# Second token half ahead of a norm by 512-column products, and the first high weight parts behind low ones 192 bytes off in a line

## The chip, the cores and the metric

The kernel runs on one core of one Trainium2 chip. The metric is device time in microseconds, the median over timed executions of the whole kernel. The core has a matrix engine (PE, with its weight loads shown as PEld), a vector engine (DVE), a scalar engine (ACT), GpSimd (POOL) and SyncE (SP), which issues most DMA transfers. PE reads its operands from SBUF and writes sums to PSUM, which has eight banks of 2 KB per partition; DVE and ACT read them from there.

## What is computed

A two-layer decoder over 256 tokens of 2048 values, in float32: a Mamba-2 layer, then an attention layer, each followed by a gated feed-forward block, and after each of the four a normalisation:

```python
def layer_norm(x, g, b):
    xf = x.astype(jnp.float32)
    mu = jnp.mean(xf, axis=-1, keepdims=True)
    var = jnp.mean(jnp.square(xf - mu), axis=-1, keepdims=True)
    return ((xf - mu) * lax.rsqrt(var + LN_EPS) * g + b).astype(x.dtype)

def conv_ffn(x, w_up, conv_w, conv_b, w_down):
    u = causal_dwconv(x @ w_up, conv_w, conv_b)
    gate, val = u[..., :D_FF], u[..., D_FF:]
    return (jax.nn.silu(gate) * val) @ w_down

    for layer in range(DEPTH):
        ...
        h = layer_norm(DEEPNORM_ALPHA * h + mix, ln_mix_g[layer], ln_mix_b[layer])
        ffn = conv_ffn(h, ffn_w_up[layer], ffn_conv_w[layer], ffn_conv_b[layer], ffn_w_down[layer])
        h = layer_norm(DEEPNORM_ALPHA * h + ffn, ln_ffn_g[layer], ln_ffn_b[layer])
```

`mix` ends in a product with `w_out` (Mamba-2) or `w_o` (attention). So each of the four norms stands behind a product into 2048 columns: `mamba_w_out` (4096 rows), `ffn_w_down` (5632 rows, twice) and `attn_w_o` (2048 rows).

## The kernel before

**Products in high and low parts.** Weights and activations are float32. A weight tile `raw` is split into a high part `hi` (ACT casts it to the rounded type that PE multiplies, L209) and the rest `lo = raw - hi` (DVE, L210). Activations are kept in the same two parts (`hT`, `yT`, `gT`, `aT`). A product is hi x hi + hi x lo + lo x hi, all added up in PSUM.

**Chunks and steps.** The weights of all layers are cut into chunks of 512 columns, and a chunk into steps; one step is one 512 KB tile. SP loads tiles in order into four `raw` buffers. `split` (L182) makes the two parts of a tile and asks for the load of another tile. There are four `hi` and four `lo` buffers, so a split waits until PE is done with an older step. PE works through the steps in an order written out by hand; other work is hung on it by `at`, `amid`, `within` and `beyond` (after a step, in its middle, within or after one half's products).

**W chunks** hold the weights still in PE. `some` (L250) goes through a step's `hi` part with 512 moving columns (L267: activations' high and low part beside each other, `x.both(k)`) and through its `lo` part with 256 (L270: the high part alone). Two steps in a row share a change: one has hi, then lo, the next lo, then hi (`kinds`, L157); in paired chunks hi, hi, lo, lo and then lo, lo, hi, hi. So PE's stream is runs of 16 or 32 L267 products and runs as long of L270 products.

**X chunks**, among them those ahead of the norms, hold the activations still and move the weights. `half(i, t, piece)` (L221) makes the products of step `i` for token half `t` (128 tokens): hi x hi (L231), hi x lo (L232), lo x hi (L236), for two row blocks, 6 products with 512 columns.

**Ahead of a norm** stand four X chunks, 512 columns each. In the last one, chunk 3, the second token half is made in two pieces of 256 columns (`second`, L239, calls `half(i, 1, 0)` and `half(i, 1, 1)`), for all its steps. Each piece has a PSUM tile of its own. The last 4 steps (TAIL; 8 in the last norm, LAST) are the tail: the first half is finished for all of them, then piece 0 for all of them, then piece 1. So the norm of the first half starts while PE works on the pieces, and that of the second half's first columns while PE works on piece 1. The chunk's first two steps (head) put both first halves ahead of both second ones. In the first three norms the weight parts of the tail's last three steps lie in `hT` (`spare`), which is free then, and the steps split behind them belong to the next chunk.

**The norm** (`class Norm`): `r` holds the residual, four tiles of 2 x 512 columns. `add` (L448) computes `r = ALPHA * r + product` on DVE out of PSUM and takes statistics; `stats` sums them up; `center` and `scale` (DVE), or `all_off` (ACT and POOL), apply them; `turn` transposes the result into `hT` by PE (L407), ACT (L411) and DVE (L412).

**Places in SBUF.** A line is 64 floats, 256 bytes. `hT`, `yT`, `gT`, `aT`, all `hi` tiles and the `lo` tiles of X chunks begin at one place in a line, called 0 here. The `lo` tiles of W chunks begin 192 bytes further (the `gap` tile lies between) and have a stretch of 32 floats between their halves, so that their weights lie at 192 and 64 in turns of two products.

**PSUM**: three `acc` tiles of two banks and two `tp` tiles of one bank. Chunk 3 has one `acc` tile for its first half, and for the pieces the first banks of the other two (in the last norm, the two `tp` tiles).

Of the kernel before, what the change touches and what calls it, by code (L numbers as in the profile page):

```python
# [18 lines left out]
F32 = mybir.dt.float32  # L19
F32R = mybir.dt.float32r  # L20
AF = mybir.ActivationFunctionType
OP = mybir.AluOpType
AX = mybir.AxisListType

P = 128
# [11 lines left out]
ALPHA = 4.0 ** 0.25  # L37
LN_EPS = 1e-5
RMS_EPS = 1e-5
NC = 512  # L40
HC = NC // 2
NEG = -1.0e30
LINE = 64
# [12 lines left out]
LAST = 8  # L56
# [35 lines left out]
def yoco_kernel(ctx: ExitStack, tc: tile.TileContext, x, lmg, lmb, lfg, lfb, x_t, columns, w, out):  # L92
    nc = tc.nc
# [10 lines left out]
    def acc_pair():  # L104
        return psum.tile([P, 2, NC], F32, tag="acc", name="acc", bufs=3)

    def tp_tile():
        return psum.tile([P, NC], F32, tag="tp", name="tp", bufs=2)
# [1 line left out]

    ident = base.tile([P, P], F32, name="ident")
    make_identity(nc, ident)
    mean = base.tile([P, P], F32R, name="mean")


    cols = base.tile([P, -(-N_COL // LINE) * LINE], F32, name="cols")
# [9 lines left out]
    steps, plan = [], chunks()  # L126

    class Chunk:

# [40 lines left out]
    def load():  # L172
# [6 lines left out]
            nc.sync.dma_start(t[:, e], w[i][:, e])  # L179
        raw_t[i] = t  # L180

    def split():  # L182
        i = pos["split"]
        pos["split"] += 1
        t = raw_t.pop(i)
        if i in spare:
            h, l = (bufs["h"][:, k:k + 2].rearrange("p k a t -> p k (a t)") for k in (spare[i], spare[i] + 2))
        else:
            h = wts.tile([P, 2, NC], F32R, tag="hi", name="hi")
            if not gap:  # L190
                gap.append(wts.tile([P, LINE * 3 // 4], F32R, tag="gap", name="gap", bufs=1))
            l = wts.tile([P, 2 * NC + LINE], F32R, tag="lo", name="lo")
            if len(gap) < 2:
                gap.append(wts.tile([P, LINE // 4], F32R, tag="gap2", name="gap2", bufs=1))
            if steps[i][0].mode == "W":
                l = l.rearrange("p (a n) -> p a n", a=2)[:, :, :NC]
            else:
                l = l[:, LINE // 4:LINE // 4 + 2 * NC].rearrange("p (a n) -> p a n", a=2)
        hi_t[i], lo_t[i] = h, l
        if steps[i][0].mode == "H":  # L200
            for a, w in enumerate((h, l)):
                v = t[:, a].rearrange("p (k n) -> p k n", k=8)
                w = w.rearrange("p a (k e n) -> p (a k) e n", e=2, n=NC // 8)
                nc.scalar.copy(w[:, :, 0], v)
                nc.vector.tensor_sub(w[:, :, 1], v, w[:, :, 0].bitcast(F32))
            return load()
        for e in ((0,), (1,)) if i < 2 else ((0, 1),):
            sl = slice(e[0], e[-1] + 1)
            nc.scalar.copy(h[:, sl], t[:, sl])  # L209
            nc.vector.tensor_sub(l[:, sl], t[:, sl], h[:, sl].bitcast(F32))  # L210
        load()
# [9 lines left out]
    def half(i, t, piece=None):  # L221

        ch, s = steps[i]
        h, l = hi_t[i], lo_t[i]
        sl = slice(0, NC) if piece is None else slice(piece * HC, (piece + 1) * HC)
        a = ch.part[t] if piece is None else ch.piece[piece]
        ts = slice(t * P, (t + 1) * P)
        for kk in range(2):
            k = 2 * s + kk
            th = ch.x.hi(k)[:, ts]  # L230
            nc.tensor.matmul(a, th, h[:, kk, sl], start=k == 0, stop=False)  # L231
            nc.tensor.matmul(a, th, l[:, kk, sl], start=False, stop=False)  # L232
        run(inner, (i, t, piece))
        for kk in range(2):
            k = 2 * s + kk
            nc.tensor.matmul(a, ch.x.lo(k)[:, ts], h[:, kk, sl], start=False, stop=k == ch.nk - 1)  # L236
        run(outer, (i, t, piece))

    def second(i):  # L239

        if steps[i][0].tail:
            half(i, 1, 0)
            half(i, 1, 1)
        else:
            half(i, 1)

    def done(i):
        hi_t.pop(i), lo_t.pop(i)
# [61 lines left out]
    def products(i):  # L310
        ch, s = steps[i]
        if ch.mode == "W":
            if s == 0:
                ch.part = []
            if s == 0 or (not ch.both and s == ch.n // 2):
                ch.part += [acc_pair() for _ in range(1 + ch.both)]
        elif s == 0:
            a = acc_pair()
            ch.part = [a[:, 0, :], a[:, 1, :]] if ch.mode == "X" else [a]
            if ch.tail:  # L320
                ch.part.pop()
                ch.piece = [tp_tile()[:, :HC] if ch.tail == LAST else acc_pair()[:, 0, :HC] for _ in range(2)]
        if ch.mode != "X":
            return whole(i)
        half(i, 0)
        if i >= ch.end - ch.tail:
            if i < ch.last:
                return splits(i)
            for q in range(2):
                for j in range(ch.end - ch.tail, ch.end):  # L330
                    half(j, 1, q)
                    if q:
                        done(j)
        elif s < ch.head - 1:
            if ch.tail:
                splits(i)
        elif s == ch.head - 1:
            for j in range(ch.first, i + 1):
                if j < i or ch.tail:
                    splits(i, 1)  # L340
                second(j)
                done(j)
        else:
            run(mid, i)
            splits(i)
            second(i)
            done(i)

    post, pre, mid, inner, outer = {}, {}, {}, {}, {}
# [11 lines left out]
    def amid(i, f, *a):  # L361
        mid.setdefault(i, []).append((f, a))
# [5 lines left out]
    def beyond(i, t, q, f, *a):  # L368

        outer.setdefault((i, t, q), []).append((f, a))  # L370
# [52 lines left out]
    class Norm:  # L423
# [24 lines left out]
        def add(self, c, h, q=None):  # L448
            r = self.r[c][:, h]
            if q is None:  # L450
                nc.vector.scalar_tensor_tensor(r, r, ALPHA, self.chs[c].part[h], op0=OP.mult, op1=OP.add)
            else:
                v = r[:, q * HC:(q + 1) * HC]
                nc.vector.scalar_tensor_tensor(v, v, ALPHA, self.chs[c].piece[q], op0=OP.mult, op1=OP.add)
            for w in (0, 1) if q is None else (q,):
                nc.vector.bn_stats(self.st[:, h, 2 * c + w, :], r[:, w * HC:(w + 1) * HC])

        def add2(self, c):
            for h in range(2):
# [133 lines left out]
    yT = bufs["y"] = mp.tile([P, DI // P, 2, S], F32R, name="yT")  # L593
    BT = mp.tile([P, NG, S], F32, name="BT")
    CT = mp.tile([P, NG, S], F32, name="CT")
    tri = base.tile([P, P], F32, name="tri")
    nc.gpsimd.memset(tri, 1.0 / NC)
    nc.vector.tensor_copy(mean, tri)
    nc.gpsimd.memset(tri, 1.0)
# [319 lines left out]
    def chain(norm, nxt=None, after=None):  # L919

        chs = norm.chs
        last = chs[3].last
        at(chs[0].first, norm.open)
        for c in range(4):
            at(max(chs[0].first, chs[c].last - 7), norm.fetch, c)
            if c < 3:
                at(chs[2].first + 3 + c, norm.fetch_gb, c)
                amid(chs[c].end, norm.add2, c) if c < 2 else beyond(chs[2].end, 0, None, norm.add2, c)
        beyond(last, 0, None, norm.add, 3, 0)
        beyond(last, 0, None, norm.stats, 0)  # L930
        if not nxt:
            return
        beyond(last, 0, None, norm.center, 0, 0)
        beyond(last, 1, 0, norm.scale, 0, 0)
        for e in range(SPARE):
            spare[last - SPARE + 1 + e] = 4 + 4 * e
        n = nxt.first

        def turn(c, h):
            turn_half(norm.r, c, h)  # L940

        beyond(last, 1, 0, norm.all_off, 1, 0)
        beyond(last, 1, 0, norm.add, 3, 1, 0)
        beyond(last - 2, 1, 1, turn, 0, 0)
        beyond(last, 1, 1, norm.add, 3, 1, 1)
        beyond(last, 1, 1, norm.stats, 1)
        beyond(last, 1, 1, norm.center, 0, 1)
        beyond(n, 0, None, norm.scale, 0, 1)
        beyond(n, 0, None, turn, 1, 0)
        beyond(n + 1, 0, None, norm.fetch_gb, 3)  # L950
        beyond(n + 1, 0, None, norm.center, 1, 1)
        beyond(n + 1, 0, None, norm.scale, 1, 1)
        within(n + 2, 0, None, turn, 0, 1)
        beyond(n + 2, 0, None, norm.all_off, 2, 0)
        beyond(n, 1, None, turn, 1, 1)
        beyond(n, 1, None, norm.center, 2, 1)
        beyond(n, 1, None, norm.scale, 2, 1)
        beyond(n + 1, 1, None, norm.all_off, 3, 0)
        beyond(n + 2, 1, None, turn, 2, 0)
        beyond(n + 2, 1, None, norm.center, 3, 1)  # L960
        beyond(n + 3, 0, None, turn, 2, 1)
        beyond(n + 3, 0, None, norm.scale, 3, 1)
        beyond(n + 4, 0, None, turn, 3, 0)
        beyond(n + 4, 1, None, turn, 3, 1)
        for c in range(4):
            at(n + 3 + c, norm.store, c)
        at(n + 6, after)
# [188 lines left out]
    def rest(h):  # L1156
# [9 lines left out]
        for q in range(2):  # L1166
            n3.norm(3, h, slice(q * HC, (q + 1) * HC))

    beyond(end, 0, None, n3.gb_psum, 3)
    beyond(end, 0, None, rest, 0)  # L1170
    beyond(end, 1, 0, n3.add, 3, 1, 0)
# [47 lines left out]
```

## Time and profile before

| | |
|---|---|
| median of 3 executions | 2513.02 us (2512.54 to 2513.26) |
| profiled execution, its own time | 2512.1 us |
| its span from first to last instruction | 2509.8 us |
| PE, PEld busy | 2497.9, 2170.8 us |
| DVE, ACT, POOL busy | 1657.9, 1365.5, 76.4 us |
| DMA | 502.59 MB, mean 200 GB/s |

A row of a timeline gives start and duration in us, engine, line, operation, what is written and read by the program's names, the shape, how many instructions follow each other, and in brackets how long the engine had been idle before and what ended that. A row of the chain of waits gives start, time and what it was. Ends of matmuls are modelled, so their pace is read from starts.

### The profile page before, as it was taken

What the parts mean: (1) busy time and instruction counts of PE and PEld (TensorE: products, weight loads), DVE (VectorE), ACT (ScalarE), POOL (GpSimd) and SP (SyncE); (2) the same over time, 40 slices, a digit from 0 to 9 for tenths busy, and PEclk for the clock granted to TensorE, in tenths of its full rate; (3) what the DMA queues carried; (4) which work ended last, traced back from release to release, by engine and by line L of the source; (5) the groups of instructions that cost most, each with busy time, mean ns of one, the idle gap of its engine ahead of it and who ended that gap; (6) DMA issues with size and microseconds to landing.
All of it is one profiled execution on the core that took longest, in us unless ns stands there. A gap on an engine that the chain in (4) does not pass through costs nothing.

```text
span 2509.8 us, 36085 instructions
## 1 busy us (share of the span) xinstructions
PE 2497.9 (100%) x13983; PEld 2170.8 (86%) x13983; DVE 1657.9 (66%) x2140; ACT 1365.5 (54%) x1790; POOL 76.4 (3%) x96
## 2 busy tenths in 40 slices
PE   9999999999999999999999999999999999999998
PEld 8888888888888888888888888888888888888887
DVE  7878888755676767675445646645767676765445
ACT  6677787643465655554334445543556555554333
POOL 0000000000200000000000200000200000000001
PEclk9999999999999999999999999999999999999999
DMA  7666655666666556656666665456666556566674
GB/s 260 207 189 205 209 191 190 205 210 220 215 203 193 193 193 193 194 185 202 210 229 204 210 193 175 161 176 227 221 192 197 194 191 194 187 200 201 199 228 161
DMA packets 141739, 502.59 MB, mean 200 GB/s; under 512 B 15856, under 2 KB 16368, under 8 KB 141568
## 3 DMA queue, kind: packets, MB, share of 16 engines
q1 hardware_dynamic: 136448, 482.92, 59.3%
q0 software_dynamic: 4832, 16.85, 2.2%
q8 instruction: 109, 1.79, 0.3%
q14 instruction: 62, 0.51, 0.1%
q10 hardware_dynamic: 288, 0.52, 0.1%
HBM read 491.77 MB, written 8.45 MB: 199 GB/s over the span
## 4 chain that ended last, share of the span: by engine, by line
PE 99%; DMA 0%; DVE 0%; SPq 0%; issue 0%; ACT 0%
PE acc L267 41%; PE acc L270 20%; PE acc L231 11%; PE acc L232 11%; PE acc L236 11%; PE acc L805 1%; PE tp L407 0%; PE tp L236 0%; PE tp L232 0%; PE tp L231 0%; DMA raw<-in_w 0%; PE tp L814 0%; PE acc L788 0%; PE tp L1084 0%; PE tp L1118 0%; PE tp L1110 0%
## 5 line engine op out<-in xcount | busy, mean ns | idle before, releaser
L210 DVE TENSOR_TENSOR lo<-raw,hi 128x1024 fp32r<-128x1024 f32 (+1 forms) x869 | 1060.0, 1225 | 722.6 <-ACT hi L209 596.4
L209 ACT CAST hi<-raw 128x1024 fp32r<-128x1024 f32 (+1 forms) x869 | 909.0, 1049 | 826.8 <-PE acc L236 366.6
L267 PE MATMUL acc<-hT,hi 128*128 128x512 f32 x4480 | 1059.0, 391 | 0.4 <-DVE hT L570 0.3
L267 PEld LDWEIGHTS acc<-hT,hi 128*128 128x128 f32 x4480 | 826.9, 188 | 165.0 <-ACT hi L209 0.9
L270 PEld LDWEIGHTS acc<-hT,lo 128*128 128x128 f32 x4480 | 538.6, 188 | 15.6 <-issue 1.2
L270 PE MATMUL acc<-hT,lo 128*128 128x256 f32 x4480 | 544.6, 277 | 0.0
L232 PE MATMUL acc<-lo,gT 128*128 128x512 f32 (+1 forms) x678 | 254.5, 378 | 0.0
L231 PE MATMUL acc<-hi,gT 128*128 128x512 f32 (+1 forms) x678 | 254.1, 377 | 0.0
L236 PE MATMUL acc<-hi,gT 128*128 128x512 f32 (+1 forms) x678 | 200.7, 377 | 0.0
L232 PEld LDWEIGHTS acc<-lo,gT 128*128 128x128 f32 x678 | 127.7, 188 | 23.3
L231 PEld LDWEIGHTS acc<-hi,gT 128*128 128x128 f32 x678 | 127.6, 188 | 23.1
L236 PEld LDWEIGHTS acc<-hi,gT 128*128 128x128 f32 x678 | 124.9, 188 | 23.6
L232 PE MATMUL acc<-lo,yT 128*128 128x512 f32 (+1 forms) x270 | 98.6, 369 | 0.0
L231 PE MATMUL acc<-hi,yT 128*128 128x512 f32 (+1 forms) x270 | 98.5, 369 | 0.0
L231 PE MATMUL acc<-hi,hT 128*128 128x512 f32 x192 | 78.8, 410 | 0.0
L236 PE MATMUL acc<-hi,yT 128*128 128x512 f32 (+1 forms) x270 | 77.7, 369 | 0.0
L232 PE MATMUL acc<-lo,hT 128*128 128x512 f32 x192 | 75.4, 393 | 0.0
L610 DVE TENSOR_TENSOR u<-u,acc 128x512 f32<-128x512 f32 x108 | 73.5, 681 | 2.3 <-ACT u L609 1.4
L637 DVE SCALAR_TENSOR_TENSOR g<-u,cols,g 128x254 f32<-128x254 f32 (+1 forms) x176 | 73.3, 478 | 2.4 <-ACT g L632 2.4
L1034 ACT CAST gT<-v 128x512 fp32r<-128x512 f32 x44 | 27.3, 621 | 84.5 <-DVE v L1033 84.5
L637 DVE SCALAR_TENSOR_TENSOR v<-u,cols,v 128x254 f32<-128x254 f32 (+1 forms) x176 | 73.2, 478 | 0.0
L469 POOL TENSOR_TENSOR rs<-rs,mhalf 128x1 f32<-128x1 f32 x8 | 7.4, 930 | 1982.1 <-DVE nb L470 1982.1
(223 smaller groups left out, 1911.3 us busy)
## 6 DMA issues: line engine op xcount, KB each, us to landing
raw<-in_w SPq DMA_DIRECT2D x880, 512.0 KB, 3.8
mA<-acum_d POOLq DMA_DIRECT2D x16, 512.0 KB, 6.1
hres<-r POOLq DMA_DIRECT2D x12, 512.0 KB, 7.1
r<-hres SPq DMA_DIRECT2D x12, 512.0 KB, 4.6
eA<-acum_d POOLq DMA_DIRECT2D x16, 128.0 KB, 7.5
r<-in_x SPq DMA_DIRECT2D x4, 512.0 KB, 5.8
gb<-in_ln_mix_g SPq DMA_DIRECT2D x8, 256.0 KB, 4.7
gb<-in_ln_mix_b SPq DMA_DIRECT2D x8, 256.0 KB, 4.9
```

The lines of the kernel that those rows point to most:

```text
L209: nc.scalar.copy(h[:, sl], t[:, sl])
L210: nc.vector.tensor_sub(l[:, sl], t[:, sl], h[:, sl].bitcast(F32))
L231: nc.tensor.matmul(a, th, h[:, kk, sl], start=k == 0, stop=False)
L232: nc.tensor.matmul(a, th, l[:, kk, sl], start=False, stop=False)
L236: nc.tensor.matmul(a, ch.x.lo(k)[:, ts], h[:, kk, sl], start=False, stop=k == ch.nk - 1)
L267: nc.tensor.matmul(banks[j], w[:, a, b, js], ch.x.both(k), start=begins, stop=ends, skip_group_check=True)
L270: nc.tensor.matmul(banks[j][:, :S], w[:, a, b, js], ch.x.hi(k), start=begins, stop=ends, skip_group_check=True)
L469: nc.gpsimd.tensor_tensor(self.rs[:, h, :], self.rs[:, h, :], mhalf[:, 0, :], op=OP.pow)
L610: nc.vector.tensor_add(dst, dst, p[:, :, :S])
L637: nc.vector.scalar_tensor_tensor(d, u[:, i % 2, :S - k], c1(self.at_w, w[n - 1 - k] + self.ia + i), d, op0=OP.mult, op1=OP.add)
L805: nc.tensor.matmul(ps[64 * q:64 * q + 64, c, j * P:(j + 1) * P], G[g]["xdt"][:, c, h * 64:(h + 1) * 64], G[g]["A", c][:, h, :], start=True ...
L1034: nc.scalar.copy(h, v[:, sl])
```

## The change

1. In chunk 3 ahead of a norm, the steps before the tail make their second half with one 512-column product in place of two of 256 columns, into a bank of their own (`ch.part[1]`): in the first three norms the second bank of piece 0's `acc` tile, in the last one the second bank of the first half's tile. The pieces sum up the tail's steps only (`k0` and `k1` say where a sum starts and ends).
2. `add_most` adds that bank to `ALPHA * r`, by a DVE instruction of 512 columns; `add` of a piece adds the piece alone. In the first three norms it stands behind the first half of the tail's last step but one, in the last norm behind the first half's sum and statistics.
3. `hi` tiles are 64 floats longer. For a W step whose `hi` part starts an L267 run behind an L270 run (`behind`), its first half lies at 192 and its second half at 0.
4. `tri` and `mean`, 512 bytes each, move from one pool to another, which makes room for the longer tiles.

```diff
-    mean = base.tile([P, P], F32R, name="mean")
...
+    def behind(i):
+
+        ch, s = steps[i]
+        if ch.mode != "W" or (ch.paired and s % 2):
+            return False
+        if ch.kinds(s)[0] == 1:
+            return True
+        ch, s = steps[i - 1]
+        return i > 0 and ch.mode == "W" and ch.kinds(s)[1] == 1
+
...
-            h = wts.tile([P, 2, NC], F32R, tag="hi", name="hi")
+            h = wts.tile([P, 2 * NC + LINE], F32R, tag="hi", name="hi")
+            if behind(i):
+                h = h[:, LINE // 2:].rearrange("p (a n) -> p a n", a=2)[:, :, LINE // 4:]
+            else:
+                h = h[:, :2 * NC].rearrange("p (a n) -> p a n", a=2)
...
+        cut = 2 * (ch.n - ch.tail)
+        k0, k1 = (cut, ch.nk) if piece is not None else (0, cut if t else ch.nk)
         for kk in range(2):
             k = 2 * s + kk
             th = ch.x.hi(k)[:, ts]
-            nc.tensor.matmul(a, th, h[:, kk, sl], start=k == 0, stop=False)
+            nc.tensor.matmul(a, th, h[:, kk, sl], start=k == k0, stop=False)
...
-            nc.tensor.matmul(a, ch.x.lo(k)[:, ts], h[:, kk, sl], start=False, stop=k == ch.nk - 1)
+            nc.tensor.matmul(a, ch.x.lo(k)[:, ts], h[:, kk, sl], start=False, stop=k == k1 - 1)
...
-                ch.part.pop()
-                ch.piece = [tp_tile()[:, :HC] if ch.tail == LAST else acc_pair()[:, 0, :HC] for _ in range(2)]
+                if ch.tail == LAST:
+                    ch.piece = [tp_tile()[:, :HC] for _ in range(2)]
+                else:
+                    a = [acc_pair() for _ in range(2)]
+                    ch.piece = [p[:, 0, :HC] for p in a]
+                    ch.part[1] = a[0][:, 1, :]
...
-                second(j)
+                half(j, 1)
...
-                nc.vector.scalar_tensor_tensor(v, v, ALPHA, self.chs[c].piece[q], op0=OP.mult, op1=OP.add)
+                nc.vector.tensor_add(v, v, self.chs[c].piece[q])
...
+        def add_most(self):
+
+            r = self.r[3][:, 1]
+            nc.vector.scalar_tensor_tensor(r, r, ALPHA, self.chs[3].part[1], op0=OP.mult, op1=OP.add)
...
-    tri = base.tile([P, P], F32, name="tri")
+    tri = mp.tile([P, P], F32, name="tri")
+    mean = mp.tile([P, P], F32R, name="mean")
...
+        if nxt:
+            beyond(last - 1, 0, None, norm.add_most)
         beyond(last, 0, None, norm.add, 3, 0)
...
+    beyond(end, 0, None, n3.add_most)
     beyond(end, 0, None, n3.gb_psum, 3)
```

More of the change, by code (lines that the diff above doesn't have):

```diff
@@ L235, in half @@
             k = 2 * s + kk
-            nc.tensor.matmul(a, ch.x.lo(k)[:, ts], h[:, kk, sl], start=False, stop=k == ch.nk - 1)
+            nc.tensor.matmul(a, ch.x.lo(k)[:, ts], h[:, kk, sl], start=False, stop=k == k1 - 1)
         run(outer, (i, t, piece))
[L239 to L245, printed above, removed]
     def done(i):
@@ L345, in products @@
             splits(i)
-            second(i)
+            half(i, 1)
             done(i)
```

## The prediction

> **What bounds the kernel now.** I read the page first (busy shares, then the chain that ended last), then the granted clock and the waits of PE, then stretches of PE's timeline.
>
> ```profile
> span 2509.8 us, 36085 instructions
> ...
> PE 2497.9 (100%) x13983; PEld 2170.8 (86%) x13983; DVE 1657.9 (66%) x2140; ACT 1365.5 (54%) x1790; POOL 76.4 (3%) x96
> ...
> PE 99%; DMA 0%; DVE 0%; SPq 0%; issue 0%; ACT 0%
> ```
> ```profile
> core 0: 2509.8 us, clock 0.998
> ```
> ```profile
> PE tp L582 <- POOL ident masks.py:199: 1.4, 1, 1.4
> PE acc L267 <- DVE hT L570: 0.3, 1, 0.3
> ```
> The chain of waits is PE for 99%, the clock is full, and the view of waits finds only 1.7 us in which PE waited idle, all of it at the start. So time changes only if PE's matmuls come at shorter distances, or if a new wait opens on PE. Ends of matmuls are modelled (a 512-column one shows 0.39 us), so I use distances between starts.
>
> The distance that a 512-column product needs when nothing disturbs it, from the chain of waits in a stretch where both token halves run 512 wide (six products from row to row):
>
> ```profile
> 1251.95 0.23 PE acc L231
> ...
> 1253.31 0.23 PE acc L231
> ...
> 1261.47 0.23 PE acc L231
> ```
> 1.36 us for six; over the 42 products to 1261.47 it is 9.52/42 = 226.7 ns.
>
> **Edit 1: the second token half by 512 columns.** One step of chunk 3 of the first ffn_w_down, in PE's timeline: six wide products, then twelve of 256 columns, then the next step.
>
> ```profile
> 1346.18 0.40 PE L231 MATMUL acc<-hi,gT 128*128 128x512 f32 x1
> ...
> 1347.57 0.28 PE L231 MATMUL acc<-hi,gT 128*128 128x256 f32 x1
> ...
> 1349.00 0.40 PE L231 MATMUL acc<-hi,gT 128*128 128x512 f32 x1
> ```
> The step takes 2.82 us: 1.39 for the six wide products and 1.43 for the twelve narrow ones (119 ns each, so 12 ns more per pair than one wide product). The wide ones also take 0.03 us more than the 1.36 above: a return from narrow to wide products costs something, which comes back below. After the change a step is two undisturbed sixes, 2.72 us: 0.10 us less. The code has 12, 18, 4 and 14 such steps (16, 22, 8 and 22 steps of the four chunks less tails of 4, 4, 4 and 8), 48 together: 4.80 us. The first two steps of a chunk put both first halves ahead, so each of the four chunks had one return fewer: 4 x 0.027 = 0.11 us off. Gain **4.7 us**. The tails keep their narrow products.
>
> The Trainium skill (TensorE: Matmul & The Clock Gate, Back-to-back issue gap) has a matmul's distance as its columns over 2.4 GHz plus about 2.5 ns. By that, an estimate, a pair of narrow products would cost only 2.5 ns more than a wide one, and the 288 pairs 0.7 us. The trace differs (12 ns a pair), and the measurement decides.
>
> Against it stands one DVE instruction more in each of the four norms, add_most: 128x512 out of PSUM, the form of L451, 0.69 us in the rows below. The three middle norms also gain a wait on PE. The second half's 512-column bank lies in the same tile as piece 0's, and in the changed program's order the first product of piece 0 waits for add_most. On DVE, add_most stands behind the last three lo splits of L210, which wait for their loads. Behind the waiting product stand all of PE's tail, the turns of the norm, and the next chunk. The rows of the third norm, then those of the first and the second:
>
> ```profile
> 1764.52 1.05 ACT L209 CAST hi<-raw 128x1024 fp32r<-128x1024 f32 x1 [1.12 <-DMA raw<-in_w]
> ```
> ```profile
> 1765.60 1.23 DVE L210 TENSOR_TENSOR lo<-raw,hi 128x1024 fp32r<-128x1024 f32 x1 [0.95 <-ACT hi L209]
> 1767.05 0.69 DVE L451 SCALAR_TENSOR_TENSOR r<-r,acc 128x512 f32<-128x512 f32 x1 [0.22 <-PE acc L236]
> ```
> ```profile
> 1766.85 0.28 PE L231 MATMUL acc<-hi,aT 128*128 128x256 f32 x1
> ```
> ```profile
> 654.98 2.50 DVE L210 TENSOR_TENSOR lo<-raw,hi 128x1024 fp32r<-128x1024 f32 x2
> ```
> ```profile
> 658.34 0.28 PE L231 MATMUL acc<-hi,yT 128*128 128x256 f32 x1
> ```
> ```profile
> 1382.89 1.23 DVE L210 TENSOR_TENSOR lo<-raw,hi 128x1024 fp32r<-128x1024 f32 x1 [0.57 <-ACT hi L209]
> ```
> ```profile
> 1385.49 0.28 PE L231 MATMUL acc<-hi,gT 128*128 128x256 f32 x1
> ```
> Third norm: the last split ends at 1766.83, so add_most would end some 0.73 us later, at 1767.56; with a handover of 0.05 us PE goes on at 1767.6. PE itself, four steps faster, would reach piece 0 about 0.38 us earlier than 1766.85, at 1766.47. The splits hang on loads (ACT waited 1.12 us for one), which start from a buffer that PE frees after this chunk's first narrow half (1.43 us, then 1.36), so they move forward only some 0.07 us. The wait is about **1.07 us**. First norm: splits end at 657.48, add_most at 658.21, PE released at 658.26 against an arrival some 0.33 us ahead of 658.34: 0.25 us. Second: 1384.90 against 1385.16: none. Together **1.3 us**. Bounds: if the loads keep pace with PE, 0.7 us (the third norm alone); if the bursts slip a little instead, 1.7 us. The DVE chain of each norm then starts level with piece 0, where it stood 0.2 us behind it (1767.05 against 1766.85), so I count no second wait.
>
> In the last norm nothing waits for add_most but the copy of the last gains (its tile is add_most's), and DVE has room:
>
> ```profile
> 2495.36 0.43 DVE L456 BATCH_NORM_STATS2 bnst<-r 128x6 f32<-128x256 f32 x1
> 2499.92 0.42 DVE L454 SCALAR_TENSOR_TENSOR r<-r,tp 128x256 f32<-128x256 f32 x1 [4.14 <-PE tp L236]
> ```
> It idled 4.14 us there for PE; 0.7 us of it goes. Without that cover the end would come 0.7 us later. The 256-column add replaces one of equal shape: nothing. Edit 1 comes to -4.7 + 1.3 = **-3.4 us** (-4.0 to -3.0).
>
> **Edit 2: the first hi parts behind lo ones, 192 bytes off.** In W chunks PE alternates between runs of L267 (hi weights, 512 columns) and L270 (lo weights, 256). The first six products of an L267 run, and seven later ones:
>
> ```profile
> 720.52 1.55 PE L267 MATMUL acc<-hT,hi 128*128 128x512 f32 x6
> ```
> ```profile
> 721.90 1.75 PE L267 MATMUL acc<-hT,hi 128*128 128x512 f32 x7
> ```
> With 0.39 us of modelled end, five distances take 1.16 us at the start, six take 1.36 us later: five settled ones would be 1.133, so a start costs **27 ns**, the same as the return from narrow to wide products in edit 1, where all addresses are at a line's start. The other change, from hi to lo, follows from the length of the cycle of 32 hi and 32 lo products:
>
> ```profile
> 709.77 7.28 PE acc L267 x32
> ...
> 1135.39 7.28 PE acc L267 x32
> ```
> ```profile
> 728.82 0.96 PE L270 MATMUL acc<-hT,lo 128*128 128x256 f32 x7
> ```
> A settled narrow product with lo weights takes (0.96 - 0.28)/6 = 113.3 ns. 39 cycles in 425.62 us are 10.913 us each; 32 x (226.7 + 113.3) ns are 10.880; so both changes cost 33 ns, and hi to lo some 7 ns. There the first lo weights already lie 192 bytes off the line in which hi and hT begin.
>
> In the changed program 180 L267 runs right behind L270 ones begin with four weight loads at 192 bytes and go on at 0 (counted in its order of instructions; four more, behind other lines, are left out). No row shows 512-column products with weights off the line. Bounds: the start costs nothing any more (-27 ns, -4.8 us), or the 27 ns are paid twice, on entry at 192 and on going back to 0 (+4.8 us). Nearest is the 7 ns change, with the same offset beside the same hT; I take 8 ns, a gain of 18.5 ns x 180 = **3.3 us**. The splits write and read the shifted tile in two runs of 512; the lo tiles of W chunks are already written so and those of X chunks in one run, both inside the L210 group, and neither engine holds PE there: no price. Moving tri and mean shifts other tiles by whole lines: no price, beyond the range's width.
>
> **The sum.** -3.4 - 3.3 = -6.7 us. The profiled execution took 2512.1 us (span 2509.8, 2.3 around it), 0.9 below the median 2513.0. So 2505.4 against its own time, **2506.3** against the median.
>
> **Rivals.** (a) *The address doesn't matter*: the 27 ns belong to the change of width alone. For: the return in edit 1 costs the same 27 ns with other tiles. Against: narrow products with all addresses at line starts take 119 ns, L270's with shifted weights 113. Only edit 1 remains: 2513.0 - 3.4 = 2509.6. This rival is also what the Trainium skill says (TensorE: Matmul & The Clock Gate, Step-by-step: what each phase is for): weight loads have a read port of their own and take no bandwidth from the running matmul; by that rule offsets do nothing. The 119 against 113 ns speak against it.
> (b) *The new wait eats edit 1*: loads slip so far in the bursts ahead of norms that PE waits 4.7 us in all, the offset works: 2513.0 - 3.3 = 2509.7. Against: even 1 us more in each of three norms makes it no more than 4.3.
> (c) *Slower*: four loads at 192 beside a moving line at 0 collide all the time, as the narrow products do (119 against 113, 6 ns each), and entry and return pay 27 ns each: 27 + 24 + 27 = 78 ns in place of 27, +51 ns x 180 = +9.2 us; with edit 1 +5.8: 2518.8. It decides from 19 ns above today's 27 on (3.4 us over 180), that is 46 ns a run. For: 512 columns with off-line weights were never seen; against: with lo, the same offset settles within 7 ns.
>
> **How the numbers follow.** Forecast 0.64, (a) 0.20, (b) 0.08, (c) 0.08. The forecast's own range is 2504.2 (both gains at their best, -4.0 and -4.8) to 2508.3 (-3.0, and half of the 3.3). The range for 8 in 10 goes on to (a) and (b) with 1.4 us for their slack, and leaves (c) out: 2503.5 to 2511.0. 0.2% (about what a measurement of this kernel can tell from no change) is 5.0 us: faster means below 2508.0, all of the forecast but its upper end, 0.61; (a), (b), that end and half-sized cases of (c) are the same, 0.33; slower 0.06.
>
> **What would show it.** Right: chunk-3 steps of 2.72 us; first six of an L267 run at about 1.53 us instead of 1.55; a wait of PE on add_most of about 1 us in the third norm, a quarter in the first, none in the second; after the last matmul the same end. Wrong: L267 starts of 1.55 (a) or more (c), or such waits of 2 us and more (b).

## The result, and the profile after

| | before | after |
|---|---|---|
| time, median of 8 runs each | 2512.94 us (2512.45 to 2513.26) | 2505.47 us (2505.05 to 2506.26) |
| profiled execution, its span | 2512.1, 2509.8 us | 2505.77, 2503.5 us |

The changed kernel takes 7.47 us less; the ratio is 0.997, with a 95% interval of 0.9962 to 0.9979. In a later group of runs it was 2505.13 against 2512.28 us, 7.15 less (0.9972, 0.9962 to 0.9983).

The page of the profile after (span, busy time of the engines, shares of the chain that ended last):

```profile
span 2503.5 us, 35513 instructions
...
PE 2490.5 (99%) x13695; PEld 2155.7 (86%) x13695; DVE 1660.2 (66%) x2144; ACT 1364.3 (54%) x1790; POOL 76.4 (3%) x96
...
PE 98%; DMA 1%; DVE 0%; ACT 0%; issue 0%; SPq 0%; ACTq 0%; DVEq 0%
```

288 matmuls fewer, and PE still sets the end. The waits of PE (total, times, longest):

```profile
PE tp L599 <- POOL ident masks.py:199: 1.4, 1, 1.4
PE acc L275 <- ACT hi L223: 1.2, 1, 1.2
```

The first is the start of before. The second is a wait for an early split; it lies in the first 20 us of the program, differs from execution to execution (from none listed to 1.9 us in those below) and belongs to neither edit. So this view shows nothing of add_most, and the rest has to come out of distances between starts.

**Steps of chunk 3.** The chain of waits where chunk 3 of the first ffn_w_down is worked (start, time to the next piece):

```profile
1337.82 0.23 PE acc L247
...
1340.54 0.23 PE acc L247
...
1343.26 0.23 PE acc L247
```

From one step's first half to the next step's it is 2.72 us, twice; before it was 2.82.

**Runs of hi products in W chunks.** The chain has each run as one piece. Two rows with 39 cycles of 32 hi (L275) and 32 lo (L278) products between them:

```profile
708.05 7.26 PE acc L275 x32
...
1132.89 7.26 PE acc L275 x32
```

424.84 us over 39 are 10.893 us a cycle, where before had 10.913: 20 ns less, once per cycle. In PE's timeline the first six of such a run take

```profile
729.68 1.53 PE L275 MATMUL acc<-hT,hi 128*128 128x512 f32 x6
```

which is the 1.53 of the prediction, 1.55 before. A start of a run costs 7 ns instead of 27. (The single starts in the traces say the same. In the kernel before, the first five distances of a run add up to 26.7 ns more than five settled ones of 226.7. In the changed kernel the first three add up to 6.6 ns more, and the rest to nothing.)

**The wait on add_most.** DVE's timeline ahead of the third norm, then PE's:

```profile
1759.08 2.50 DVE L224 TENSOR_TENSOR lo<-raw,hi 128x1024 fp32r<-128x1024 f32 x2 [1.08 <-ACT hi L223]
1761.50 0.68 DVE L473 SCALAR_TENSOR_TENSOR r<-r,acc 128x512 f32<-128x512 f32 x1
```
```profile
1761.48 0.61 PE L252 MATMUL acc<-hT,aT 128*128 128x512 f32 x2
1762.23 0.39 PE L247 MATMUL acc<-hi,aT 128*128 128x256 f32 x1
1762.46 0.28 PE L248 MATMUL acc<-lo,aT 128*128 128x256 f32 x1
```

Two wide products need 0.45 us; here piece 0 starts 0.75 after the first of them, just behind the end of add_most (1762.18). Its own distance is 0.22 instead of 0.11. Together PE loses 0.41 us: there is a wait, though the view of waits does not list it. The same reading of the second norm gives 0.15, and the first has none: there DVE had 0.64 us to spare behind add_most,

```profile
655.49 0.68 DVE L473 SCALAR_TENSOR_TENSOR r<-r,acc 128x512 f32<-128x512 f32 x1
656.80 0.69 DVE L463 SCALAR_TENSOR_TENSOR r<-r,acc 128x512 f32<-128x512 f32 x1 [0.64 <-PE acc L252]
```

and in the last norm it idles for PE as before, 3.54 us instead of 4.14:

```profile
2484.14 0.68 DVE L473 SCALAR_TENSOR_TENSOR r<-r,acc 128x512 f32<-128x512 f32 x1
...
2493.60 0.42 DVE L466 TENSOR_TENSOR r<-r,tp 128x256 f32<-128x256 f32 x1 [3.54 <-PE tp L252]
```

From the start of that last 256-column sum to the end it is 9.9 us, before as well (2499.92 to 2509.8).

A wait of another kind stands in the tail of the last norm. The split of the chunk's last step hangs on its load. Here are that split on ACT and on DVE, and PE's products of that step:

```profile
2478.26 1.05 ACT L223 CAST hT<-raw 128x1024 fp32r<-128x1024 f32 x1 [2.53 <-DMA raw<-in_w]
```
```profile
2479.35 1.22 DVE L224 TENSOR_TENSOR hT<-raw,hT 128x1024 fp32r<-128x1024 f32 x1 [2.35 <-ACT hT L223]
```
```profile
2480.10 0.39 PE L247 MATMUL acc<-hT,gT 128*128 128x512 f32 x1
2480.62 0.50 PE L248 MATMUL acc<-hT,gT 128*128 128x512 f32 x1
2480.96 0.40 PE L247 MATMUL acc<-hT,gT 128*128 128x512 f32 x1
```

The lo part is whole at 2480.57, and L248, which reads it, starts at 2480.62: 0.52 us behind the product before, and its own distance is 0.34, where 0.23 each would do. PE loses 0.41 us, again without a row in the view of waits. In the kernel before, that lo part was whole at 2485.42 and its product came at 2487.08, so there was room. Other executions below have this wait too (e3 0.96 us, e6 0.82, e9 0.85), the rest have none.

### The profile page after: what moved, and what is told of

Same layout as the page of the kernel before. It is cut to its first block, busy times and chain, and to the rows that moved or that the text cites. A ratio compares the mean times of both kernels' runs of the same rounds, so it can differ in the third digit from the quotient of the medians.

```text
span 2503.5 us, 35513 instructions
## 1 busy us (share of the span) xinstructions
PE 2490.5 (99%) x13695; PEld 2155.7 (86%) x13695; DVE 1660.2 (66%) x2144; ACT 1364.3 (54%) x1790; POOL 76.4 (3%) x96
## 4 chain that ended last, share of the span: by engine, by line
PE 98%; DMA 1%; DVE 0%; ACT 0%; issue 0%; SPq 0%; ACTq 0%; DVEq 0%
PE acc L275 41%; PE acc L278 20%; PE acc L247 11%; PE acc L252 11%; PE acc L248 11%; DMA raw<-in_w 1%; PE acc L823 1%; PE tp L419 0%; PE tp L832 0%; PE acc L806 0%; PE tp L1104 0%; PE tp L1138 0%; PE tp L1130 0%; PE tp L252 0%; PE tp L247 0%
## 5 line engine op out<-in xcount | busy, mean ns | idle before, releaser
L275 PE MATMUL acc<-hT,hi 128*128 128x512 f32 x4480 | 1055.9, 391 | 1.2 <-ACT hi L223 1.2
L275 PEld LDWEIGHTS acc<-hT,hi 128*128 128x128 f32 x4480 | 826.6, 188 | 162.8 <-ACT hi L223 2.2
L278 PEld LDWEIGHTS acc<-hT,lo 128*128 128x128 f32 x4480 | 538.7, 188 | 15.6 <-issue 1.2
L278 PE MATMUL acc<-hT,lo 128*128 128x256 f32 x4480 | 544.4, 277 | 0.0
L247 PE MATMUL acc<-hi,gT 128*128 128x512 f32 (+1 forms) x670 | 260.5, 389 | 0.0
L248 PE MATMUL acc<-lo,gT 128*128 128x512 f32 (+1 forms) x670 | 260.3, 389 | 0.0
L252 PE MATMUL acc<-hi,gT 128*128 128x512 f32 (+1 forms) x670 | 206.0, 389 | 0.0
L248 PEld LDWEIGHTS acc<-lo,gT 128*128 128x128 f32 x670 | 125.8, 188 | 26.0
L247 PE MATMUL acc<-hi,yT 128*128 128x512 f32 (+1 forms) x246 | 95.4, 388 | 0.0
L248 PE MATMUL acc<-lo,yT 128*128 128x512 f32 (+1 forms) x246 | 95.3, 388 | 0.0
L248 PE MATMUL acc<-lo,hT 128*128 128x512 f32 x192 | 75.5, 393 | 0.0
L252 PE MATMUL acc<-hi,yT 128*128 128x512 f32 (+1 forms) x246 | 75.3, 388 | 0.0
```

Of the source, the lines that this page charges most:

```text
L247: nc.tensor.matmul(a, th, h[:, kk, sl], start=k == k0, stop=False)
L275: nc.tensor.matmul(banks[j], w[:, a, b, js], ch.x.both(k), start=begins, stop=ends, skip_group_check=True)
L278: nc.tensor.matmul(banks[j][:, :S], w[:, a, b, js], ch.x.hi(k), start=begins, stop=ends, skip_group_check=True)
```

## The experiments

Each run was timed beside the kernel before in the same group: 2512.47 us in the first group (e1 to e4), 2512.49 in the second (e5_add_early to e8), 2512.28 in the third. Differences below are taken within the group. All intervals of the ratios are about 0.001 to either side; the medians lie closer together than that, so for the small steps the traces decide and the times are the check.

**One edit at a time.** Edit 1 alone (e1) is the changed kernel with the condition of the offset taken out:

```diff
-            if behind(i):
+            if False:
```

> The changed kernel with the first hi parts of W chunks back at the start of a line: edit 1 alone. My theory (both edits act, each through distances on PE): chunk-3 steps stay at 2.72 us, starts of L275 runs go back to about 27 ns, PE's waits on add_most stay near 0.5 us together; 4.7 - 0.6 = 4.1 us less than the kernel before, about 2508.8 us. Rival 'the address does not matter': as the changed kernel, 2505.5 us. Rival 'the new waits eat the columns' gain': as the kernel before, 2512.9 us.

Measured: 2508.86 us (2507.93 to 2510.62), 3.61 less than before; ratio 0.9986 (0.9977 to 0.9995). The cycle of hi and lo products, in its chain of waits:

```profile
708.62 7.28 PE acc L275 x32
...
1134.24 7.28 PE acc L275 x32
```

425.62/39 = 10.913 us, the cycle of before to the nanosecond. Here the third norm's wait was longer than in the changed kernel's profile, as PE's timeline shows:

```profile
1763.09 0.61 PE L252 MATMUL acc<-hT,aT 128*128 128x512 f32 x2
1764.71 0.39 PE L247 MATMUL acc<-hi,aT 128*128 128x256 f32 x1 [1.01 <-DVE r L473]
1764.93 0.28 PE L248 MATMUL acc<-lo,aT 128*128 128x256 f32 x1
```

1.62 - 0.45 + 0.11 = 1.28 us (the row counts only 1.01, from the modelled end of the product before). 4.7 - 1.28 = 3.4 is near the 3.61 measured; the 0.5 us that I had expected for the wait, from the profile of after, was a miss. Neither rival holds: edit 1 gives about half, and the wait does not eat it.

Edit 2 alone (e2) is the kernel before with the longer `hi` tile, `behind` and the moved `tri` and `mean`; `half`, `products` and the norm stay as they were.

> The kernel before with the first hi parts at 192 bytes (and tri and mean moved): edit 2 alone. My theory: 20 ns less at each of 180 starts, 3.6 us, about 2509.3 us; chunk-3 steps stay at 2.82 us. Rival 'the address does not matter': 2512.9 us. Rival 'all of the gain is the offset's': 2505.5 us.

Measured: 2509.07 us (2508.77 to 2509.76), 3.40 less; ratio 0.9986 (0.9978 to 0.9995). Its chain (its hi line is L281):

```profile
709.03 7.26 PE acc L281 x32
...
1133.87 7.26 PE acc L281 x32
```

424.84/39 = 10.893 us, the cycle of after. The address matters, and by 180 x 20 ns = 3.6 us. The two alone add up to 7.0 us; together they gave 7.5 and 7.2.

**Where in the line.** Four kernels differ from the changed one only in where a `hi` tile behind lo products lies.

```diff
-                h = h[:, LINE // 2:].rearrange("p (a n) -> p a n", a=2)[:, :, LINE // 4:]
+                h = h[:, LINE:].rearrange("p (a n) -> p a n", a=2)                                           # e3
+                h = h[:, LINE * 3 // 4:LINE * 3 // 4 + 2 * NC].rearrange("p (a n) -> p a n", a=2)            # e4
+                h = h.rearrange("p (a n) -> p a n", a=2)[:, :, LINE // 2:]                                   # e7
+                h = h[:, LINE // 4:]                                                                         # e8
+                h = bass.AP(tensor=h.tensor, offset=h.offset, ap=[list(h.ap[0]), [NC + LINE * 3 // 4, 2], [1, NC]])
```

> The changed kernel with the first hi parts 256 bytes off in their tile instead of 192 (the second half of that tile stays at 2304 bytes): so they lie elsewhere, but at the same place of a 256-byte line as in the kernel before. My theory (only the place within 256 bytes counts): starts of L275 runs take about 27 ns again, 2505.5 + 3.6 = 2509.1 us. Rival 'any move off the old address does it': starts stay near 7 ns, 2505.5 us.

> The changed kernel with both parts of the first hi tile at 192 bytes, so that eight loads of a run lie off the line instead of four. My theory (only the loads right behind the lo products matter, a settled 512-column product takes 226.7 ns wherever its weights lie): same as the changed kernel, 2505.5 us within 0.5, starts near 7 ns. Rival 'products with weights off the line cost more and only four of them hide it': the fifth to eighth distances rise by 5 ns or more each, 180 x 4 x 5 ns = 3.6 us more, 2509.1 us. Rival 'going back to 0 costs and was hidden in the start': that cost shows one tile later, up to 27 ns x 180, 2510 us.

> The changed kernel with the first hi parts at 128 bytes in their line instead of 192; the second parts stay at 0. Theory 'slip' (a start costs 16 cycles of 2.4 GHz for each 64 bytes that the first loads lie ahead of the next line's start: 64 at 0 bytes, 16 at 192): 32 cycles, 13.3 ns a start, 180 x 6.7 ns = 1.2 us more than the changed kernel, 2506.7 us. Rival 'any place off the start of a line does': 6.6 ns, 2505.5 us. Rival 'only 192 does, because the lo loads before lie there': 26.7 ns, 2509.1 us.

> The changed kernel with the first hi parts at 64 bytes in their line instead of 192; the second parts stay at 0. Theory 'slip': 48 cycles, 20 ns a start, 2.4 us more than the changed kernel, 2507.9 us. Rival 'any place off the start of a line does': 2505.5 us. Rival 'only 192 does': 2509.1 us.

Their chains of waits, in this order, 39 cycles between the two rows of each:

```profile
709.66 7.28 PE acc L275 x32
...
1135.28 7.28 PE acc L275 x32
```
```profile
711.16 7.29 PE acc L275 x32
...
1137.04 7.29 PE acc L275 x32
```
```profile
709.45 7.27 PE acc L275 x32
...
1134.81 7.27 PE acc L275 x32
```
```profile
710.36 7.29 PE acc L276 x32
...
1136.24 7.29 PE acc L276 x32
```

A start's cost is 6.6 ns (the changed kernel's) plus what the cycle is longer than 10.893 us. The fourth column is worked out from it: 3.61 (edit 1 alone, measured, so the first row fits by construction) + 180 x (26.7 - cost).

| first hi part, second (bytes) | cycle, us | a start, ns | less than before, worked out, us | measured, us |
|---|---|---|---|---|
| 0, 0 (before, e1) | 10.913 | 27 | 3.6 | 3.61 |
| 256 = 0, 0 (e3) | 10.913 | 27 | 3.6 | 3.76 (2508.71 us) |
| 192, 0 (after) | 10.893 | 7 | 7.2 | 7.47, 7.15 |
| 128, 0 (e7) | 10.907 | 20 | 4.8 | 4.81 (2507.68 us) |
| 64, 0 (e8) | 10.920 | 33 | 2.4 | 2.46 (2510.03 us) |
| 192, 192 (e4) | 10.920 | 33 | 2.4 | 3.20 (2509.27 us) |

e3 moves the tile farther than the change does, and the whole gain is gone: what counts is not the move but the place within 256 bytes. e7 and e8 refute my first law for the size (13 and 20 ns expected, 20 and 33 found): 64 bytes are worse than no offset at all. From 192 down to 64 bytes a start rises by 13 ns per 64 bytes; whole tiles at 0 do not fit that line, and why is open. In time, e4 is 0.8 us better than worked out; its runs spread from 2508.47 to 2512.13 us, and this too stays open.

e4 goes against my theory. I had taken it that a settled wide product needs 226.7 ns wherever its weights lie. PE's timeline of e4, the first 8 and the first 12 products of one run (two windows that end at different places),

```profile
721.92 2.00 PE L275 MATMUL acc<-hT,hi 128*128 128x512 f32 x8
...
721.92 2.92 PE L275 MATMUL acc<-hT,hi 128*128 128x512 f32 x12
```

and the same of the changed kernel:

```profile
718.78 1.98 PE L275 MATMUL acc<-hT,hi 128*128 128x512 f32 x8
...
718.78 2.89 PE L275 MATMUL acc<-hT,hi 128*128 128x512 f32 x12
```

The row of eight products is some 10 to 20 ns longer, that of twelve 30 (the eighth product's modelled end makes up 9 ns of the first: by starts, eight products are 6 ns dearer). In single starts: with weights at 192 the distances repeat 226, 229, 232 ns, twice over, so that products there cost 2.2 ns more than settled ones for as long as they stay; going back to 0 then takes 236, 228, 232 and 231, 20 ns in all. Of the two rivals of that expectation each had a part. The changed kernel leaves 192 after four loads, and its fourth distance is 227 already; why going back costs nothing there and 20 ns after eight is not shown.

**The lo side.** The same rule asked of the other change of run: lo tiles with their first part at 64 and the second at 192 bytes, where they had 192 and 64 (on top of e5 below). This is e9.

```diff
-                gap.append(wts.tile([P, LINE * 3 // 4], F32R, tag="gap", name="gap", bufs=1))
+                gap.append(wts.tile([P, LINE // 4], F32R, tag="gap", name="gap", bufs=1))
...
-                gap.append(wts.tile([P, LINE // 4], F32R, tag="gap2", name="gap2", bufs=1))
+                gap.append(wts.tile([P, LINE * 3 // 4], F32R, tag="gap2", name="gap2", bufs=1))
...
-                l = l[:, LINE // 4:LINE // 4 + 2 * NC].rearrange("p (a n) -> p a n", a=2)
+                l = l[:, LINE * 3 // 4:LINE * 3 // 4 + 2 * NC].rearrange("p (a n) -> p a n", a=2)
```

> The same early add_most, and the lo tiles of W chunks moved so that their first part lies at 64 bytes and the second at 192 (it was 192, then 64). Theory 'the place of the first loads decides at every change of run': a change from hi to lo costs more than its 7 to 9 ns, up to the 33 ns that hi parts at 64 bytes cost, 180 x 25 ns = 4.5 us more than the run before, 2509 us. Rival 'in runs of 256 columns the place matters less, and lo parts alternate between both places anyway': the same as the run before, 2504.6 us.

Measured: 2507.83 us (2507.33 to 2508.71), 3.64 more than e5 in the same group. Its chain:

```profile
708.31 7.26 PE acc L275 x32
...
1133.93 7.26 PE acc L275 x32
```

The cycle is 20 ns longer at 10.913 us, with hi runs of 7.26 as in the changed kernel: so a change from hi to lo costs 27 ns in place of 7, and 180 x 20 ns are the 3.6 us. The place counts in runs of 256 columns as well.

**The wait on add_most.** First its cost, by reading the bank twice (e6): the second pass adds 0 times the bank.

```diff
             nc.vector.scalar_tensor_tensor(r, r, ALPHA, self.chs[3].part[1], op0=OP.mult, op1=OP.add)
+            nc.vector.scalar_tensor_tensor(r, self.chs[3].part[1], 0.0, r, op0=OP.mult, op1=OP.add)
```

> The changed kernel with the read of add_most's bank done twice (a second pass that adds 0 times the bank), so that PE's bank comes free 0.68 us later in each middle norm. My theory: PE waits about 0.3 us in the first norm (0.43 us were to spare), 0.15 + 0.68 in the second, 0.4 + 0.68 in the third: 1.65 us more, 2507.1 us. Rival 'the handover is hidden, and the odd distances there have another cause': 2505.5 us. Rival 'DVE's whole chain of the norm moves with it and PE's turns wait too': 0.7 us in each of three norms beyond that, up to 2509 us.

Measured: 2506.67 us (2505.18 to 2508.16), 5.82 less than before, so 1.3 to 1.65 more than the changed kernel's 7.15 and 7.47. PE's timeline in the third norm:

```profile
1760.86 0.61 PE L252 MATMUL acc<-hT,aT 128*128 128x512 f32 x2
1762.75 0.38 PE L247 MATMUL acc<-hi,aT 128*128 128x256 f32 x1 [1.28 <-DVE r L474]
```

Piece 0 now waits for the second pass, L474: with its own late distance 1.55 us (1.89 - 0.45 + 0.11). The first norm waited 0.2 us (expected 0.3), the second 0.05, less than I expected, its last split being early in that execution. So the handover is on PE's path. These waits add up to 1.8 us, 0.7 more than the changed kernel's have on average (1.1, below), and the last norm's wait for its split was 0.82 us here; how much of the rise each makes is not told apart.

Then without the wait (e5): add_most two steps earlier, ahead of the last two lo splits on DVE.

```diff
-            beyond(last - 1, 0, None, norm.add_most)
+            beyond(last - 3, 0, None, norm.add_most)
```

> The changed kernel with add_most issued two steps earlier (at last - 3), so that on DVE it stands ahead of the last two lo splits instead of behind them. My theory: what is left of PE's wait on add_most (about 0.15 us in the second norm, 0.4 us in the third, by the distances of the changed kernel's last L252 and first piece-0 product) goes away: 0.5 us less, 2505.0 us, and the distance of 524 ns in the third norm falls to 227. Rival 'PE would wait there for something else, the splits or their loads': distances stay, 2505.5 us or, if a split that now stands behind add_most comes late, up to 0.7 us more.

Measured: 2504.61 us (2503.58 to 2505.81), 7.88 less than before, but not in one group with the changed kernel. So both ran once more, side by side:

> The changed kernel once more, beside the next run on the same chip. Every theory: the same 2505.5 us within 0.5. For the wait on add_most: the six executions seen so far that have it at last - 1 waited 0.4 to 1.26 us in the third norm, so this one waits somewhere between, and none or up to 0.4 us in the second, none in the first.

> The changed kernel with add_most at last - 3, once more. My theory: no wait on add_most in any norm; against the changed kernel in the same runs it is 0.4 to 1.3 us less, as long as the wait that the changed kernel has in the third norm, so about 2504.6 us. Rival 'the time that PE no longer waits there it waits a little later': 2505.5 us, and the distances after the tail grow.

Measured: 2505.13 us (2505.00 to 2506.06, 7 runs) for the changed kernel, 2504.19 us (2503.53 to 2504.79, 6 runs) with the early add_most. No run of the one lies within the runs of the other; 0.94 us. The third norm in PE's timeline, changed kernel first, then the early add_most (and its DVE):

```profile
1760.52 0.61 PE L252 MATMUL acc<-hT,aT 128*128 128x512 f32 x2
1761.96 0.39 PE L247 MATMUL acc<-hi,aT 128*128 128x256 f32 x1 [0.82 <-DVE r L473]
```
```profile
1760.46 0.61 PE L252 MATMUL acc<-hT,aT 128*128 128x512 f32 x2
1760.91 0.28 PE L247 MATMUL acc<-hi,aT 128*128 128x256 f32 x1
1761.02 0.28 PE L248 MATMUL acc<-lo,aT 128*128 128x256 f32 x1
```
```profile
1757.05 0.68 DVE L473 SCALAR_TENSOR_TENSOR r<-r,acc 128x512 f32<-128x512 f32 x1
1758.07 1.23 DVE L224 TENSOR_TENSOR lo<-raw,hi 128x1024 fp32r<-128x1024 f32 x1 [0.34 <-ACT hi L223]
```

1.44 - 0.45 + 0.11 = 1.1 us of wait there, none here: two wide products in 0.45, a narrow one in 0.11. add_most now runs in a pause in which DVE waits for a split anyway (for ACT's hi part, and ACT had waited 1.11 us for the load). What the wait cost came back nearly whole, 0.94 of 1.1 us, and the rival that PE would wait later instead falls. This version, 8.1 us under the kernel before, is faster than both.

## Why the prediction was right

2506.3 us was forecast, 2505.47 measured: the right mechanisms, and 0.8 us more gain than the sum of 6.7. Two parts of the agreement were luck, and are called so below.

- **Bound.** PE's starts set the end before and after, and both gains are distances between starts. The profiles of the single edits show each gain where it was put.
- **Steps of 2.72 instead of 2.82 us**: measured so. The 4.7 us hold. (The section of the Trainium skill that the prediction sets beside this, TensorE: Matmul & The Clock Gate, Back-to-back issue gap, gives that distance for an isolated matmul and says that in a stream of weight loads and matmuls both set it; the prediction left that condition out, and its sum does not rest on it.)
- **The wait on add_most, 1.3 us**: right in kind, a little too large. Third norm, 1.07 forecast: 0.41 in the profile of after, but 1.09 in the second profile of the same kernel, and 1.28 in e1; in the seven profiled executions with one add_most at that place (after twice, e1, e3, e4, e7, e8) 0.41 to 1.28, 1.0 on average. The step says that the splits hang on loads, and these land differently in every execution; one profile could not have shown the spread. First norm, 0.25 forecast: none in any of the seven. There the step let the loads move forward by only a part of PE's gain; they moved by more than PE did: add_most ended 0.43 us ahead of piece 0 (656.17 against 656.60). Second norm, none forecast: none in five, 0.15 and 0.38 us in two. On the seven's average the term is 1.1 us.
- **PE's wait for the last split in the last norm**: the prediction had no such term. In the kernel before there was none, in the seven executions two have it (after 0.41, e3 0.96 us), 0.2 us on average. So all new waits come to the 1.3 us forecast, but not where they were forecast: that the total fits was luck.
- **A start at 192 bytes, 8 ns**: 6.6 ns, and 3.6 us over 180 starts where 3.3 were forecast. The row that I went by, the change from hi to lo with the same offset, was the right neighbour; its own cost of 7 to 9 ns stayed as it was. But the reason given was too simple: offsets of 64 bytes, or of 192 on all eight loads, are dearer than none. That four loads at 192 pay nothing on going back to 0, where eight pay 20 ns, no step of the prediction gave a reason for: the choice was lucky there.
- **The same end**: yes, DVE's pause in the last norm took add_most in.
- **The sum.** With the measured sizes, 4.7 - 1.1 - 0.2 + 3.6 = 7.0 us, what the single edits add up to, against 7.15 and 7.47 measured. So 0.3 of the 0.8 us are named, by the starts. The rest stays open; it is no larger than what the medians of before differ from group to group (2512.28 to 2512.94 us), and the waits may be put too high, as five of the seven profiled executions took longer than the median of their kernel.
- **Rival (a), the address doesn't matter**: refuted by e1, e2 and e3 together; it would have had e2 at no change. With it falls, for this kernel, what the prediction drew from the Trainium skill (TensorE: Matmul & The Clock Gate, Step-by-step: what each phase is for: weight loads through a read port of their own take no bandwidth from the running matmul), namely that offsets do nothing: the place of the weights alone moved a start between 7 and 33 ns. Whether the two reads disturb each other is not shown by that.
- **Rival (b), the waits eat edit 1**: it needed 4.7 us of waits; the largest sum of the norms' new waits in one of the seven executions was 2.1 (e3, 1.16 on add_most and 0.96 on the last split).
- **Rival (c), slower**: it needed 46 ns a run; 7 were found. Its idea, that loads off the line beside a moving operand at 0 keep costing, is what e4 shows, at 2.2 ns a product and not 6. By the starts, the other places tried would have given edit 2 a third of its gain (128 bytes), nothing (256), or a loss of 1.2 us (64, or 192 in both parts).

## What to carry to other kernels

Where PE sets the end and waits for nothing, measure the distance between matmul starts, per kind of product and at each change of kind, against the settled distance; here some 20 ns at each of 180 changes brought about as much as 288 saved matmuls less their new waits (3.40 and 3.61 us, each edit alone). Try the place of the first weights within 256 bytes in steps of 64, each by itself: here the sign of the effect could not be told from one place. And when the reader of a PSUM bank becomes a condition for PE, issue it early, once its data are whole, ahead of instructions of the same engine that wait for loads: one line moved was worth 0.9 us here.

## What the runs showed of the hardware that was not expected

- A run of 512-column products behind one of 256 starts at a cost that depends on where its first four weight loads lie within 256 bytes: 27 ns at 0, 33 at 64, 20 at 128, 7 at 192, and 27 again at 256. That weight loads and the reads of the moving operand get into each other's way, and slip until they don't, would fit; no run tells that from another cause.
- A wide product with weights at 192 beside a moving operand at 0 is not settled at 226.7 ns: it takes 228.9 on average, and leaving this state after eight products costs 20 ns, after four nothing.
- Piece 0's first product shows a distance of 0.22 us instead of 0.11 whenever PE had to wait in front of it: a stall costs some 0.1 us more than its own length, which the view of waits does not count. A 512-column product behind the stall in the last norm shows the same (0.34 instead of 0.23). Of the 0.41 us in the third norm of after the view listed nothing, and of the 1.28 us in e1 it counted 1.01: it measures from the modelled end of the product before.
- The products behind that stall in the last norm, all 512 columns wide, take 236, 229, 232 and 231 ns in after and, to 1 ns, in e6, much as a run with weights at 0 does in its second to fifth distance behind a 256-column run (236, 228, 232 and 231). So such distances do not need a change of width.
